# Sums of squares by VectorE and one ones matmul per half in the first stage of a decoder layer

## The chip, the cores and the metric

The kernel runs on one NeuronCore of a Trainium2 chip. The metric is the device time of one execution in microseconds (us). TensorE does matmuls, VectorE (DVE) and ScalarE (ACT) do elementwise work, GpSimd (POOL) does elementwise work on SBUF, and SyncE (SP) issues nearly all DMA transfers. Each engine runs its own instructions strictly in the order in which the program has them.

## The reference, cut to what matters

One layer: a token mixer with three branches and a ConvFFN after it, 1024 tokens of width 1024, all in float32. The change concerns only the start of the mixer: the RMS norm of the input and the first products with the input projection.

```python
def rms_norm(x, g):
    y = x * rsqrt(mean(x * x, axis=-1) + 1e-6)
    return y * g

h = rms_norm(x, norm_mix_pre)
z = h @ w_in                        # (1024, 7424), all branches from one projection
zr = z_rwkv + (token_shift(z_rwkv) - z_rwkv) * mu_shift
r, k, v, dw, da, dg = split(zr)     # 3 x 1024, 64, 64, 128 columns
w_log = -softplus(-(w0 + tanh(dw) @ w_up_decay)) - 0.5
a = sigmoid(a0 + da @ w_up_a)
g = sigmoid(dg) @ w_up_g
```

## The kernel before, in words

Everything lies transposed: channels on the 128 partitions, tokens along the row. x is held as eight tiles `xr[k]` of 128 channels x 1024 tokens, and the tokens are worked in two halves of 512 (`t0` = 0 and 512). A float32 operand of a matmul is split in two reduced parts: a rounded "high" part (`hh` of the input, `whi` of a weight) and the rest (`hl`, `wlo`). One product then takes three matmuls of 128x512 (`mm3`, L168 to L170): high by high, low by high, high by low. One projection of 128 columns (`gemm`) is 8 channel blocks of these, 24 matmuls into one PSUM bank. Banks come from the pool `psg` under two tags, `g0` and `g1`, two banks each; a weight's class `c` (0 or 1) says which tag, and also which SBUF buffers it uses (four each of `whi` and `wlo`, so one whole projection of 8 blocks, two blocks to a buffer).

The norm's factor 1/rms of a token is the same for all channels, so the first projections are taken from x * g without it, and the factor `xrs` is multiplied onto the PSUM result (`scaled`, L283) before it is evacuated (`shifted`, L309 to L315: ScalarE writes (1-mu) * z, VectorE adds mu times z shifted by a token). The sum over channels for the mean of squares runs over partitions: TensorE multiplies a 128x128 tile of 1/1024 (`ones`) in full float32 with the squares (`xsq`), block by block, into the bank `px` (L263). The profile shows such a full-float32 matmul as two instructions.

The function `start` runs the first stage in this order: `plain(0, first)` makes `hh` and `hl` of half 0, the squares, eight ones matmuls, and k and v of half 0 (the columns of heads 0 and 1), channel block by channel block; then the two small projections, decay and rate (`lu`, weight block 32) and gate (`gr`, block 33), of half 0; then `plain(512, after=last_mm[0])`, which has no projection: `hh`, `hl`, squares and eight ones matmuls of half 1; then `normed(0)`, which multiplies the factor onto x of half 0 and splits it anew; then decay, gate, k and v of half 1, for which the weights of k and v are loaded and split a second time. Then tanh and sigmoid, and the gate's own product: eight blocks p, each for both halves, three matmuls each (`gl`), copied out by ScalarE (`st`, L325) and stored to `d_g`. `normed(512)` comes last, tied to the copies. The code after it takes the next heads' k and v from the normed `hh` and `hl`.

The order on each engine is set by a scheduler that places the instructions by its own costs within what the code's dependences and the hints of `later` (an order without a wait) allow; so the rows on an engine are not simply the order of the code.

Of the kernel before, what the change touches and what calls it, by code (L numbers as in the profile page):

```python
# [9 lines left out]
F32 = mybir.dt.float32  # L10
FR = mybir.dt.float32r
AF = mybir.ActivationFunctionType
# [32 lines left out]
def trunk_kernel(ctx: ExitStack, tc: tile.TileContext, xT, memT, pvec, w_in, w_kv, w_upd, w_upg,  # L45
# [49 lines left out]
    for lo in (0, 64):  # L95
        s = slice(lo, lo + 64)
        V.tensor_scalar(cent[s], ident[s, lo:lo + 64], 1.0, -1.0 / 64, op0=ALU.mult, op1=ALU.add)
# [75 lines left out]
    def gemm(ws, rhs, width=512, behind=None, ps=None, log=None):  # L173
# [4 lines left out]
        for k in range(n):  # L178
# [3 lines left out]
            if log is not None:  # L182
                log.append(last_mm[0])
        return ps
# [58 lines left out]
    def plain(t0, ws=(), after=None):  # L243

        ts_ = slice(t0, t0 + 512)
        px = pss.tile([P, 512], F32, name="px", tag="s")
        pj = [psg.tile([P, 512], F32, name="psg", tag=f"g{w.c}") for w in ws]
        pin = phase[1][-1]
        for k in range(KC):
            x, hi = xr[k][:, ts_], hh[:, k, ts_]  # L250
            sq = wp.tile([P, 512], F32, name="xsq", tag="st", bufs=3)
            i = A.activation(hi, x, AF.Identity, scale=col("g_mix_pre", k))
            if t0:
                later(i, pin)
            V.scalar_tensor_tensor(hl[:, k, ts_], x, col("g_mix_pre", k), hi.bitcast(F32), op0=ALU.mult,
                                   op1=ALU.subtract)
            if k % 2 or t0:
                i = A.activation(sq, x, AF.Square)
                if t0:
                    later(i, pin)  # L260
            else:
                V.tensor_tensor(sq, x, x, op=ALU.mult)
            mm = PE.matmul(px, ones, sq, start=k == 0, stop=k == KC - 1)  # L263
            if after is not None:
                later(mm, after)
            for w, ps in zip(ws, pj):
                mm3(ps, w[k], (hi, hl[:, k, ts_]), k == 0, k == KC - 1)
        rstd(xrs_[:, ts_], px, 0)
        return pj

# [96 lines left out]
    def start():  # L367
# [5 lines left out]
        kv0 = rw.tile([P, 2, T], F32, name="kv0", tag="X00")  # L373
        SP.dma_start(gr[:, 1], w_upg)
        evs = [shifted(8, kv0[:, 0]), shifted(16, kv0[:, 1])]
        for ev, ps in zip(evs, plain(0, first)):
            scaled(ev, 0, ps)
        lo_ = [(shifted(24, u), load_w(w_in[32], KC, c=0)),
               (shifted(25, gr[:, 0]), load_w(w_in[33], KC, c=1))]
        for ev, ws in lo_:  # L380
            scaled(ev, 0, gemm(ws, hrhs(0)))
        hi_on_act[0] = False
        plain(512, after=last_mm[0])
        normed(0)
        for ev, ws in lo_:
            scaled(ev, 512, gemm(ws, hrhs(512)))
        for c, ev in enumerate(evs):
            scaled(ev, 512, gemm(load_w(w_in[16 + 8 * c], KC, c=c), hrhs(512)))
# [4 lines left out]
        act(gr[:, 0], gr[:, 0], AF.Sigmoid)  # L393
# [1273 lines left out]
```

## Time and profile before

| what | us |
|---|---|
| median of 3 runs | 2056.73 (2052.93 to 2056.75) |
| the profiled execution, its own time | 2058.67 |
| its span from the first to the last instruction | 2056.8 |
| TensorE busy | 2000.2 (97% of the span) |
| VectorE, ScalarE, GpSimd busy | 1378.4, 1073.6, 804.4 |

The mean granted TensorE clock of the execution is 0.995 of full speed. A time in a row of the profile counts from the start of the span. A row of the timeline gives start, duration, engine, line of the code, operation, output and inputs, a count, and in brackets the idle time of the engine before it with what ended it. The stage that is changed lies in the first 92 us of the span.

### The profile page before, as it was taken

How to read it: one execution, taken by the hardware profiler on the slowest of the kernel's cores; microseconds unless marked ns; L12 is line 12 of the kernel's file. 1: busy time of each engine (PE TensorE's matmuls, PEld its weight loads, DVE VectorE, ACT ScalarE, POOL GpSimd, SP SyncE). 2: the span in 40 equal slices, each digit the busy share in tenths (PEclk: the TensorE clock that was granted, in tenths of full speed). 3: DMA queues.
4: the chain of work that ended last, by engine and by line, in shares of the span. 5: the costliest groups of instructions: out<-in, count | busy, mean ns of one | idle time of the engine just before them, and what ended most of it. 6: DMA issues, size and time to landing. Idle time of an engine off the chain costs nothing. (4 is left out here: it accounts for less than half of the span.)

```text
span 2056.8 us, 34070 instructions
## 1 busy us (share of the span) xinstructions
PE 2000.2 (97%) x12246; PEld 1558.2 (76%) x12246; DVE 1378.4 (67%) x2204; ACT 1073.6 (52%) x2249; POOL 804.4 (39%) x883
## 2 busy tenths in 40 slices
PE   8999999999999999999999999999999999999997
PEld 5777767786778667776778887877678888877886
DVE  6567537663568357734596552768889888867798
ACT  7575338723773358434567343545544554444544
POOL 4521213121222121111122355655579888832441
PEclk9999999999999999999999999999999999999999
DMA  4412112120212121212525543645332222169776
GB/s 152 136 42 75 66 36 86 58 93 22 88 62 83 36 90 40 90 63 89 193 92 189 157 136 106 191 129 164 97 95 87 85 80 82 67 198 260 166 183 150
DMA packets 176714, 221.84 MB, mean 108 GB/s; under 512 B 16544, under 2 KB 128288, under 8 KB 176544
## 3 DMA queue, kind: packets, MB, share of 16 engines
q1 hardware_dynamic: 163616, 204.44, 30.7%
q0 software_dynamic: 11856, 14.16, 4.2%
q8 instruction: 97, 1.59, 0.3%
q10 hardware_dynamic: 1072, 1.05, 0.2%
q14 instruction: 73, 0.60, 0.1%
HBM read 170.30 MB, written 49.28 MB: 107 GB/s over the span
## 5 line engine op out<-in xcount | busy, mean ns | idle before, releaser
L132 POOL TENSOR_TENSOR wlo<-wraw,whi 128x256 fp32r<-128x256 f32 x472 | 412.7, 884 | 940.7 <-ACT whi L129 774.5
L168 PE MATMUL psg<-hh,whi 128*128 128x512 f32 x928 | 380.1, 410 | 2.6 <-DVE kv L315 2.6
L170 PE MATMUL psg<-hh,wlo 128*128 128x512 f32 x928 | 376.3, 406 | 0.4
L169 PE MATMUL psg<-hl,whi 128*128 128x512 f32 x928 | 375.5, 405 | 0.0
L129 ACT CAST whi<-wraw 128x256 fp32r<-128x256 f32 x472 | 182.5, 403 | 227.6 <-PE psg L169 105.7
L168 PEld LDWEIGHTS psg<-hh,whi 128*128 128x128 f32 x928 | 174.6, 188 | 43.1 <-DVE kv L315 3.8
L170 PEld LDWEIGHTS psg<-hh,wlo 128*128 128x128 f32 x928 | 174.2, 188 | 43.2 <-POOL wlo L132 5.9
L169 PEld LDWEIGHTS psg<-hl,whi 128*128 128x128 f32 x928 | 174.6, 188 | 39.4 <-issue 3.6
L1011 POOL TENSOR_TENSOR wt<-a,wt 128x256 fp32r<-128x256 f32 x136 | 156.7, 1176 | 35.6 <-ACT wt L1010 35.6
L168 PE MATMUL psd<-f,u 128*128 128x512 f32 x292 | 114.7, 393 | 3.1 <-ACT u L1405 2.4
L169 PE MATMUL psd<-f,u 128*128 128x512 f32 x292 | 114.6, 393 | 0.6 <-DVE f L1409 0.6
L170 PE MATMUL psd<-f,u 128*128 128x512 f32 x292 | 114.1, 392 | 0.0
L170 PE MATMUL psf<-h2h,wt 128*128 128x512 f32 x272 | 105.9, 389 | 1.0 <-POOL wt L1011 1.0
L169 PE MATMUL psf<-h2l,wt 128*128 128x512 f32 x272 | 105.8, 389 | 0.0
L168 PE MATMUL psf<-h2h,wt 128*128 128x512 f32 x272 | 105.8, 389 | 0.0
L1025 DVE SCALAR_TENSOR_TENSOR d<-z,pv,d 128x1023 f32<-128x1023 f32 x68 | 101.1, 1491 | 2.2
L1011 POOL TENSOR_TENSOR wt<-s,wt 128x256 fp32r<-128x256 f32 x68 | 80.3, 1201 | 3.4 <-ACT wt L1010 2.1
L686 DVE TENSOR_TENSOR HV<-ph,Hd 64x128 f32<-64x128 f32 x112 | 32.4, 289 | 72.2 <-PE ph L640 48.1
L168 PE MATMUL psf<-t,wt 128*128 128x512 f32 x204 | 79.4, 389 | 0.0
L169 PE MATMUL psf<-t,wt 128*128 128x512 f32 x204 | 79.4, 389 | 0.0
L170 PE MATMUL psf<-t,wt 128*128 128x512 f32 x204 | 79.4, 389 | 0.0
L1023 ACT ACTIVATE d<-z,pv 128x1024 f32<-128x1024 f32 x34 | 42.4, 1246 | 67.6 <-DVE z L1102 51.9
(425 smaller groups left out, 4747.0 us busy)
## 6 DMA issues: line engine op xcount, KB each, us to landing
wraw<-in_w_in SPq DMA_DIRECT2D x240, 128.0 KB, 2.4
a<-in_w_fup SPq DMA_DIRECT2D x128, 128.0 KB, 2.4
d_zg<-st SPq DMA_DIRECT2D x48, 256.0 KB, 2.7
wraw<-in_w_fup SPq DMA_DIRECT2D x80, 128.0 KB, 2.5
fw<-in_w_fdn SPq DMA_DIRECT2D x33, 256.0 KB, 4.3
fraw<-d_f SPq DMA_DIRECT2D x33, 256.0 KB, 4.5
wraw<-in_w_prwkv SPq DMA_DIRECT2D x64, 128.0 KB, 2.4
wraw<-in_w_o SPq DMA_DIRECT2D x64, 128.0 KB, 2.5
```

What stands on the lines that cost most here:

```text
L129: last_whi[0] = A.copy(hi, src).ins
L132: (V if lo_on_dve[0] else G).tensor_tensor(lo, src, hi.bitcast(F32), op=ALU.subtract)
L168: first = PE.matmul(ps, wh, xh, start=start, stop=False)
L169: PE.matmul(ps, wh, xl, start=False, stop=False)
L170: last_mm[0] = PE.matmul(ps, wl, xh, start=False, stop=stop).ins
L686: ready = V.tensor_tensor(HV[q, :, c + 1, e], ph[q], Hd[q], op=ALU.add).ins
L1011: low = eng.tensor_tensor(w[1][:, us], src[u], w[0][:, us].bitcast(F32), op=ALU.subtract)
L1023: A.activation(d, z, AF.Identity, scale=col("cw2", j), bias=col("cb", j))
L1025: V.scalar_tensor_tensor(d[:, n:], z[:, :T - n], col(cw, j), d[:, n:], op0=ALU.mult, op1=ALU.add)
```

## The change

Three things are changed in the first stage.

1. The squares of the eight channel blocks are added up by VectorE into a tile `xsum`, one per half, and one ones matmul per half takes the sum over partitions (`x_norm`). Before there were eight ones matmuls per half.
2. k and v are taken from the unnormed operand in both halves (`plain(512, first, ...)`), before gate and decay, with the weights still in SBUF. The norm's factor of half 0 is made after channel block 3 of half 1 (`amid`), that of half 1 after block 3 of the gate projection of half 0. Gate now comes before decay.
3. The gate's sigmoid and split are done for each half by itself, the gate's products run over half 0 first, and both `normed` come after. The table of ScalarE functions for the sigmoid is loaded once, after the second norm factor. The tile `cent` is made later in the code.

```diff
-    def plain(t0, ws=(), after=None):
+    def plain(t0, ws, sum_, amid=None):
 
         ts_ = slice(t0, t0 + 512)
-        px = pss.tile([P, 512], F32, name="px", tag="s")
         pj = [psg.tile([P, 512], F32, name="psg", tag=f"g{w.c}") for w in ws]
-        pin = phase[1][-1]
         for k in range(KC):
             x, hi = xr[k][:, ts_], hh[:, k, ts_]
-            sq = wp.tile([P, 512], F32, name="xsq", tag="st", bufs=3)
-            i = A.activation(hi, x, AF.Identity, scale=col("g_mix_pre", k))
-            if t0:
-                later(i, pin)
+            sq = wp.tile([P, 512], F32, name="xsq", tag="st", bufs=3) if k else sum_
+            A.activation(hi, x, AF.Identity, scale=col("g_mix_pre", k))
             V.scalar_tensor_tensor(hl[:, k, ts_], x, col("g_mix_pre", k), hi.bitcast(F32), op0=ALU.mult,
                                    op1=ALU.subtract)
             if k % 2 or t0:
-                i = A.activation(sq, x, AF.Square)
-                if t0:
-                    later(i, pin)
+                A.activation(sq, x, AF.Square)
             else:
                 V.tensor_tensor(sq, x, x, op=ALU.mult)
-            mm = PE.matmul(px, ones, sq, start=k == 0, stop=k == KC - 1)
-            if after is not None:
-                later(mm, after)
+            if k:
+                V.tensor_tensor(sum_, sum_, sq, op=ALU.add)
             for w, ps in zip(ws, pj):
                 mm3(ps, w[k], (hi, hl[:, k, ts_]), k == 0, k == KC - 1)
-        rstd(xrs_[:, ts_], px, 0)
+            if amid is not None and k == 3:
+                amid()
         return pj
+
+    def x_norm(t0, sum_):
+        px = pss.tile([P, 512], F32, name="px", tag="s")
+        later(PE.matmul(px, ones, sum_, start=True, stop=True), last_mm[0])
+        rstd(xrs_[:, t0:t0 + 512], px, 0)
...
         kv0 = rw.tile([P, 2, T], F32, name="kv0", tag="X00")
+        sums = rw.tile([P, 2, 512], F32, name="xsum", tag="X10")
+        evs = [shifted(8, kv0[:, 0]), shifted(16, kv0[:, 1])]
+        made = {}
+
+        def kv_done(n, t0):
+            x_norm(t0, sums[:, n])
+            for ev, ps in zip(evs, made[n]):
+                scaled(ev, t0, ps)
+
+        made[0] = plain(0, first, sums[:, 0])
+        made[1] = plain(512, first, sums[:, 1], partial(kv_done, 0, 0))
         SP.dma_start(gr[:, 1], w_upg)
-        evs = [shifted(8, kv0[:, 0]), shifted(16, kv0[:, 1])]
-        for ev, ps in zip(evs, plain(0, first)):
-            scaled(ev, 0, ps)
-        lo_ = [(shifted(24, u), load_w(w_in[32], KC, c=0)),
-               (shifted(25, gr[:, 0]), load_w(w_in[33], KC, c=1))]
-        for ev, ws in lo_:
-            scaled(ev, 0, gemm(ws, hrhs(0)))
+        lo_ = [(shifted(25, gr[:, 0]), load_w(w_in[33], KC, c=1)),
+               (shifted(24, u), load_w(w_in[32], KC, c=0))]
         hi_on_act[0] = False
-        plain(512, after=last_mm[0])
+        split_w(gr[:, 1], gl[:, 2], gl[:, 3])
+
+        def gate(t0):
+            s = slice(t0, t0 + 512)
+            act(gr[:, 0, s], gr[:, 0, s], AF.Sigmoid)
+            split(gr[:, 0, s], gl[:, 0, s], gl[:, 1, s])
+
+        for t0, _ in HALVES:
+            for n, (ev, ws) in enumerate(lo_):
+                asked = partial(kv_done, 1, 512) if n == 0 and t0 == 0 else None
+                scaled(ev, t0, gemm(ws, hrhs(t0), amid=asked))
+                if asked:
+                    table(SIGMOID)
+                if n == 0:
+                    gate(t0)
+        for t0, _ in HALVES:
+            for p in range(8):
+                ps_ = slice(p * P, (p + 1) * P)
+                ws = Ws([(gl[:, 2, ps_], gl[:, 3, ps_])])
+                ws.c = 1
+                spilled(d_g[p])(t0, gemm(ws, lambda k: (gl[:, 0, t0:t0 + 512], gl[:, 1, t0:t0 + 512])))
         normed(0)
-        for ev, ws in lo_:
-            scaled(ev, 512, gemm(ws, hrhs(512)))
-        for c, ev in enumerate(evs):
-            scaled(ev, 512, gemm(load_w(w_in[16 + 8 * c], KC, c=c), hrhs(512)))
+        normed(512, spills)
```

How the change moves instructions is shown at three places. From the matmul that stands next on TensorE behind 268 projection and gate matmuls (the kernel before starts it at 91.69 us) the order of both programs is the same on TensorE; ahead of it both have the same 268 and differ in the ones matmuls and the order.

First, TensorE where the half 1 ones matmuls stood. Before, behind the last matmuls of gate's half 0 (bank `psg_408`) and ahead of decay's half 1 (`psg_504`):

```order
L170 MATMUL psg_408<-hh_143,wlo_375 128x512
L263 MATMUL px_437<-xsq_438,ones_85 128x512
L263 MATMUL px_437<-xsq_443,ones_85 128x512
L263 MATMUL px_437<-xsq_448,ones_85 128x512
L263 MATMUL px_437<-xsq_453,ones_85 128x512
L263 MATMUL px_437<-xsq_458,ones_85 128x512
L263 MATMUL px_437<-xsq_463,ones_85 128x512
L263 MATMUL px_437<-xsq_468,ones_85 128x512
L263 MATMUL px_437<-xsq_473,ones_85 128x512
L168 MATMUL psg_504<-hh_143,whi_331 128x512
```

And now, at the seam from v of half 1 (`psg_314`) to gate of half 0 (`psg_466`), up to that gemm's second block pair:

```order
L165 MATMUL psg_314<-hh_141,whi_196 128x512
L166 MATMUL psg_314<-hl_142,whi_196 128x512
L167 MATMUL psg_314<-hh_141,wlo_197 128x512
L165 MATMUL psg_466<-hh_141,whi_416 128x512
L166 MATMUL psg_466<-hl_142,whi_416 128x512
L167 MATMUL psg_466<-hh_141,wlo_417 128x512
```

The eight ones matmuls in a row are gone; gate of half 0 follows v of half 1 at once, and its bank is one of the two of tag `g1`, both of which v's halves still hold. The two remaining ones matmuls stand inside gemms, behind block 3.

Second, VectorE in the same stretch. Before, from the last blocks of half 0 to the first evacuation:

```order
L255 SCALAR_TENSOR_TENSOR hl<-xr_147,pv,hh 128x512 x4
L262 TENSOR_TENSOR xsq<-xr_147 128x512
L283 TENSOR_TENSOR psg<-psg,xrs 128x512 x2
L274 SCALAR_TENSOR_TENSOR xr_145<-xr_145,pv,xrs 128x512
L311 COPY zc<-psg 128x1
L315 SCALAR_TENSOR_TENSOR kv_224<-psg,pv,kv_224 128x511
```

And now, from the last blocks of half 1 to the first evacuation (`xr_145` is here the tile of blocks 4 to 7):

```order
L257 TENSOR_TENSOR xsum<-xsum,xsq 128x512
L250 SCALAR_TENSOR_TENSOR hl<-xr_145,pv,hh 128x512
L257 TENSOR_TENSOR xsum<-xsum,xsq 128x512
L744 TENSOR_SCALAR cent<-ident 64x64
L281 TENSOR_TENSOR psg<-psg,xrs 128x512 x2
L272 SCALAR_TENSOR_TENSOR xr_143<-xr_143,pv,xrs 128x512
L309 COPY zc<-psg 128x1
L313 SCALAR_TENSOR_TENSOR kv_221<-psg,pv,kv_221 128x511
```

The evacuation of k and v of half 0 moved behind all sixteen `hl` of both halves and the fourteen additions; half of `cent` stands there too.

Third, ScalarE while the gate's products are copied out. Before:

```order
L325 COPY st<-psg 128x512 x2
L277 CAST hh<-xr_146 128x512
L325 COPY st<-psg 128x512 x2
L277 CAST hh<-xr_146 128x512
```

And now:

```order
L323 COPY st<-psg 128x512 x2
L275 CAST hh<-xr_144 128x512
L412 CAST ld<-lu 64x1024
L323 COPY st<-psg 128x512
L412 CAST la<-lu 64x1024
L323 COPY st<-psg 128x512 x2
L275 CAST hh<-xr_144 128x512
L434 ACTIVATE sp<-kv_221,pv 128x512
L323 COPY st<-psg 128x512
```

The tanh, the two casts of its result and the squares `sp` of the next step, which stood ahead of the gate's copies, now stand between them.

More of the change, by code (lines that the diff above doesn't have):

```diff
@@ L94, in trunk_kernel @@
     smask = const.tile([P, 512], F32, name="smask")
-    for lo in (0, 64):
-        s = slice(lo, lo + 64)
-        V.tensor_scalar(cent[s], ident[s, lo:lo + 64], 1.0, -1.0 / 64, op0=ALU.mult, op1=ALU.add)
     G.memset(mstrict, 1.0)
@@ L171, in mm3, with gemm @@
         return first
-    def gemm(ws, rhs, width=512, behind=None, ps=None, log=None):
+    def gemm(ws, rhs, width=512, behind=None, ps=None, log=None, amid=None):
         if ps is None:
@@ L257, in plain @@
             if k % 2 or t0:
-                i = A.activation(sq, x, AF.Square)
-                if t0:
-                    later(i, pin)
+                A.activation(sq, x, AF.Square)
             else:
                 V.tensor_tensor(sq, x, x, op=ALU.mult)
-            mm = PE.matmul(px, ones, sq, start=k == 0, stop=k == KC - 1)
-            if after is not None:
-                later(mm, after)
+            if k:
+                V.tensor_tensor(sum_, sum_, sq, op=ALU.add)
             for w, ps in zip(ws, pj):
                 mm3(ps, w[k], (hi, hl[:, k, ts_]), k == 0, k == KC - 1)
-        rstd(xrs_[:, ts_], px, 0)
-        return pj
+            if amid is not None and k == 3:
+                amid()
+        return pj
+    def x_norm(t0, sum_):
+        px = pss.tile([P, 512], F32, name="px", tag="s")
+        later(PE.matmul(px, ones, sum_, start=True, stop=True), last_mm[0])
+        rstd(xrs_[:, t0:t0 + 512], px, 0)
     def normed(t0, behind=None):
@@ L392, in start @@
             V.tensor_tensor(l[o], u[q], l[q].bitcast(F32), op=ALU.subtract)
-        act(gr[:, 0], gr[:, 0], AF.Sigmoid)
-        split(gr[:, 0], gl[:, 0], gl[:, 1])
-        split_w(gr[:, 1], gl[:, 2], gl[:, 3])
-        for p in range(8):
-            ps_ = slice(p * P, (p + 1) * P)
-            ws = Ws([(gl[:, 2, ps_], gl[:, 3, ps_])])
-            ws.c = 1
-            ev = spilled(d_g[p])
-            for t0, _ in HALVES:
-                ev(t0, gemm(ws, lambda k: (gl[:, 0, t0:t0 + 512], gl[:, 1, t0:t0 + 512])))
-        normed(512, spills)
         return kv0
@@ L729, in fill_to @@
         return filled[n - 1]
-    table(SIGMOID)
     first_kv = start()
+    for lo in (0, 64):
+        s = slice(lo, lo + 64)
+        V.tensor_scalar(cent[s], ident[s, lo:lo + 64], 1.0, -1.0 / 64, op0=ALU.mult, op1=ALU.add)
     kv = group_kv(0, [first_kv])
```

## The prediction

> **What bounds the kernel now.** I read the page first, for the engine that is never free.
>
> ```profile
> PE 2000.2 (97%) x12246; PEld 1558.2 (76%) x12246; DVE 1378.4 (67%) x2204; ACT 1073.6 (52%) x2249; POOL 804.4 (39%) x883
> ```
>
> TensorE is busy 97% of the span, so whatever time its stream gains or loses at the start moves all that follows. The page's slices are 51 us wide and too coarse for the stage, so next I cut it at the points where TensorE's work changes kind: half 0 with its ones matmuls, the half 1 ones matmuls, the 96 matmuls of half 1, the seam to the gate, and on to 91.69, the first matmul that stands alike in both programs.
>
> ```profile
> core 0: us, PE busy (x) PEld busy (x) DVE busy (x) ACT busy (x) POOL busy (x), PEclk, DMA share, GB/s
> 5.31:36.74 31.43, 30.89 (x112) 21.76 (x113) 18.04 (x26) 21.28 (x41) 17.83 (x20) 1.00 0.67 221
> 36.74:47.41 10.67, 8.43 (x17) 3.38 (x16) 10.48 (x19) 9.60 (x17) 0.00 (x0) 0.84 0.01 2
> 47.41:69.75 22.34, 22.34 (x98) 18.00 (x97) 19.20 (x25) 12.50 (x16) 19.26 (x24) 1.00 0.20 59
> 69.75:75.30 5.55, 2.15 (x8) 1.23 (x7) 3.26 (x4) 3.80 (x9) 3.32 (x5) 1.00 0.33 96
> 75.30:91.69 16.39, 16.39 (x70) 12.75 (x70) 6.38 (x11) 12.97 (x24) 0.27 (x1) 1.00 0.66 240
> ```
>
> Two stretches hold no projection work or little: 10.67 us in which only ones matmuls run, and 5.55 us at the seam to the gate with 2.15 busy. The timeline says what they are made of.
>
> ```profile
> 16.83 1.02 PE L263 MATMUL px<-xsq,ones 128*128 128x512 f32 x2
> 19.08 1.02 PE L263 MATMUL px<-xsq,ones 128*128 128x512 f32 x2
> 41.72 6.25 PE L263 MATMUL px<-xsq,ones 128*128 128x512 f32 x10 [2.24 <-ACT xsq L258]
> 71.20 0.50 PE L169 MATMUL psg<-gl 128*128 128x512 f32 x1 [0.95 <-DVE gl L123]
> 75.30 0.50 PE L168 MATMUL psg<-gl 128*128 128x512 f32 x1 [2.45 <-ACT st L325]
> 97.58 0.39 PE L168 MATMUL psg<-hh,whi 128*128 128x512 f32 x1
> 104.38 0.39 PE L168 MATMUL psg<-hh,whi 128*128 128x512 f32 x1
> ```
>
> From 97.58 to 104.38 thirty matmuls start: 0.2267 us each. From 16.83 to 19.08 go six of them (1.36) and one ones matmul, two instructions: 0.89. The block from 36.74 is eight of these, 7.1 us, and 3.5 us in which TensorE waits for ScalarE's squares.
>
> **What is removed.** Fourteen ones matmuls, 14 x 0.89 = 12.5 us of TensorE; the 3.5 us of waiting in their block; and at the seam 5.55 less eight matmuls (1.8), 3.7 us, if the gate's operand is ready in time. That is 19.7 us, and no more can be won. Four of the five table loads after the first also go, and the second load and split of the weights of k and v: eight transfers and eight pairs on POOL, all beside the path, where SP and POOL waited for room.
>
> **What is paid: VectorE feeds TensorE.** The fourteen additions go to the engine that makes `hl`, which every second matmul of a block waits for.
>
> ```profile
> L255 DVE SCALAR_TENSOR_TENSOR hl<-xr,pv,hh 128x512 fp32r<-128x512 f32 x16 | 12.9, 836 | 3.9 <-ACT hh L252 3.7
> L262 DVE TENSOR_TENSOR xsq<-xr 128x512 f32<-128x512 f32 x4 | 3.3, 822 | 1.0 <-DMA xr<-in_xT 1.0
> L97 DVE TENSOR_SCALAR cent<-ident 64x64 f32<-64x64 f32 x2 | 1.7, 830 | 0.0
> 8.99 0.75 DVE L255 SCALAR_TENSOR_TENSOR hl<-xr,pv,hh 128x512 fp32r<-128x512 f32 x1 [2.94 <-ACT hh L252]
> 9.66 0.68 DVE L262 TENSOR_TENSOR xsq<-xr 128x512 f32<-128x512 f32 x1
> 10.26 0.74 DVE L255 SCALAR_TENSOR_TENSOR hl<-xr,pv,hh 128x512 fp32r<-128x512 f32 x1
> 13.30 1.23 DVE L262 TENSOR_TENSOR xsq<-xr 128x512 f32<-128x512 f32 x1
> 14.45 4.16 DVE L255 SCALAR_TENSOR_TENSOR hl<-xr,pv,hh 128x512 fp32r<-128x512 f32 x4
> 37.46 2.07 DVE L255 SCALAR_TENSOR_TENSOR hl<-xr,pv,hh 128x512 fp32r<-128x512 f32 x3
> 12.83 4.57 POOL L132 TENSOR_TENSOR wlo<-wraw,whi 128x256 fp32r<-128x256 f32 x4 [0.28 <-ACT whi L129]
> ```
>
> No addition of SBUF tiles of this size is in the trace; the nearest row is the square, also a tensor by tensor of 128x512. Up to 8.99 nothing changes (the second block of x lands then). From there to the last `hl` of half 1 the order has 15 `hl`, 3 squares, 13 additions and one `cent`. At the means, 15 x 0.836 + 16 x 0.822 + 0.83 = 26.5 us: the last `hl` is ready at 35.5. The bounds lie in the rows below: start to start, with POOL idle, `hl` takes 2.07 / 3 = 0.69 and the square 10.26 - 9.66 = 0.60, which gives 20.8 us; beside POOL's `wlo` `hl` takes 4.16 / 4 = 1.04 and one square 1.23, which gives 36.1 us. I take the means, since in the new stretch POOL works about half the time (the splits of k and v, `gl` and the splits for gate and decay).
>
> The Trainium skill says why the two sets of rows differ, in "GPSIMD Engine Reference", Specifications: POOL shares its SBUF interfaces with VectorE and meets "contention with DVE instructions in a 2-port perf mode or with two SBUF inputs". Each addition has two SBUF inputs, so by this rule the change adds work of the exposed kind; the 1.04 against 0.69 agrees. By it alone the sum would lie toward the upper bound.
>
> Five matmuls follow the last `hl`: TensorE is through with k and v at 36.6, where before (36.74) it had done as many projection matmuls, k, v, decay and gate of half 0.
>
> **What is paid: the bank.** Gate of half 0 needs a bank of tag `g1`, and both are v's. It is freed by a chain on VectorE behind the last addition.
>
> ```profile
> 28.87 1.30 DVE L283 TENSOR_TENSOR psg<-psg,xrs 128x512 f32<-128x512 f32 x2 [9.65 <-ACT xrs L200]
> 31.91 0.73 DVE L315 SCALAR_TENSOR_TENSOR kv<-psg,pv,kv 128x511 f32<-128x511 f32 x1
> 10.31 5.14 SPq L234 DMA_DIRECT2D xr<-in_xT  x9
> DMA to landing us min/median/max: 3.2/5.7/6.0
> L274 DVE SCALAR_TENSOR_TENSOR xr<-xr,pv,xrs 128x512 f32<-128x512 f32 x16 | 13.1, 857 | 0.0
> ```
>
> Before, the same chain (two `scaled`, one `xr`, two evacuations) runs from 28.87 to 32.64, 3.77 us. Now: last addition 35.5 + 0.8, `cent` 0.8, chain 3.8: the bank is free at 40.9, and TensorE idles 4.3 us; everything on TensorE is queued behind it. What is late next? The factor itself is not: half 0's sum is complete by 8.99 + 8 `hl` + 10 others + `cent`, about 25, and ScalarE is through with half 1 some three blocks ahead of VectorE, since it has three buffers of squares. Nor is x: the last transfer is issued by 15.5 and lands by 21.5. Seven `xr` (7 x 0.857 = 6.0) stand ahead of the second evacuation: 40.9 + 6.0 + 3.8 = 50.7, and its bank is wanted only by half 1 of gate, from 53.6.
>
> **Gate and decay.** 96 matmuls, 21.8 us, one ones matmul, 0.9, and the clock.
>
> ```profile
> 40.00:45.00 5.00, 3.28 (x5) 1.35 (x6) 5.00 (x10) 3.95 (x9) 0.00 (x0) 0.79 0.01 3
> 45.00:50.00 5.00, 5.00 (x16) 3.03 (x15) 4.26 (x7) 4.82 (x7) 0.63 (x2) 0.87 0.00 0
> 75.00:80.00 5.00, 4.70 (x18) 3.25 (x19) 1.64 (x4) 3.73 (x8) 0.57 (x1) 1.00 0.59 209
> ```
>
> After the idle 2.24 us the granted clock was 0.79 and 0.87 for two windows, 5 x 0.21 + 5 x 0.13 = 1.7 us; after the 2.45 at the seam it stayed 1.00. I take 0.9, with 0 and 1.7 as ends. So 40.9 + 21.8 + 0.9 + 0.9 = 64.5.
>
> The page "TensorE: Matmul & The Clock Gate" of the Trainium skill, in Part 1, gives half rate after an idle window of about 3.4 us and full rate again after about as long a busy one; that would be an estimated 1.7 for the new gap. The gap of 2.24 with its 0.79 fits it only loosely.
>
> **The gate's stage.** 76 matmuls stand between there and 91.69's instruction: 17.2 us. The gate's operand took 8.9 us from its scaling (62.23) to its split (69.73 + 1.41); now half 0's comes to 50.7 + 8.9 = 59.6, before 64.5, and half 1's to 68, while eight products and ten matmuls of the next k fill up to 72. So the 3.7 us do go.
>
> ```profile
> 62.23 0.69 DVE L283 TENSOR_TENSOR psg<-psg,xrs 128x512 f32<-128x512 f32 x1
> 69.73 1.41 DVE L123 TENSOR_TENSOR gl<-gr,gl 128x1024 fp32r<-128x1024 f32 x1 [1.34 <-ACT gl L122]
> L325 ACT COPY st<-psg 128x512 f32<-128x512 f32 x16 | 9.3, 588 | 3.4 <-PE psg L170 2.8 <-DMA d_g<-st 0.5
> L277 ACT CAST hh<-xr 128x512 fp32r<-128x512 f32 x16 | 9.4, 618 | 0.0
> L424 ACT ACTIVATE sp<-kv,pv 128x512 fp32r<-128x512 f32 x2 | 1.4, 722 | 0.9 <-DVE gl L123 0.6 <-DVE kv L315 0.3
> L200 ACT ACTIVATE lu<-lu 64x1024 f32<-64x1024 f32 x1 | 1.1, 1060 | 2.1 <-DVE lu L315 2.1
> L391 ACT CAST la<-lu 64x1024 fp32r<-64x1024 f32 x1 | 1.1, 1051 | 0.0
> L309 ACT ACTIVATE lu<-psg,omu 128x512 f32<-128x512 f32 x2 | 1.4, 679 | 3.6 <-DVE psg L283 3.6
> ```
>
> But ScalarE, which empties the banks, now has more between the copies: 16 x 0.588 + 8 x 0.618 + 2 x 0.722 + 1.06 + 2 x 1.05 + 2 x 0.68 = 20.3 us. Neighbours overlap by up to 0.1, some 3 us over thirty, so the wait beyond TensorE's 17.2 is between 0 and 3.1; I take 1.5. That ends the stage at 64.5 + 17.2 + 1.5 = 83.2.
>
> **The sum.** 91.69 - 83.2 = 8.5 us earlier, and behind it TensorE's order is unchanged: 19.7 removed, and paid back 11.2, mostly by the wait for `hl` and for the bank. The profiled execution would go from 2058.67 to 2050.2. The median of the runs, 2056.73, lies 1.9 below that execution; from it, 2048.2. A measurement of this kernel tells about 0.2%, 4.1 us, from no change.
>
> **The rivals.**
>
> 1. VectorE runs free of POOL. At the lower bound the last `hl` comes 5.7 earlier, gain 14.2, time 2042.5. For it: POOL's weight splits of k and v for half 1 are gone, and it waits for buffers that TensorE holds. Against it: in half 0 the rows with 1.04 stand in just this stretch. Chance 0.24.
> 2. VectorE is contended throughout. The last `hl` comes 9.6 later, and all of the gain is eaten: loss 1.1, time 2057.8, no change that can be measured. For it: denser work on VectorE meets POOL more often, and one of the four squares was slow. Against it: POOL was idle from 17.4 to 22.3, for `gl`'s weights landed no earlier. Chance 0.18, most of it for something between this and the forecast.
> 3. Slower: TensorE's clock. Fed block by block with short gaps from 9 to 36 us and then left idle for 4.3, TensorE is granted half speed and stays there while the banks of tag `g1` let it start and stop. It decides where the loss exceeds 8.5 + 4.1 = 12.6 us, which is 25 us of wall time at half speed; for all of gate and decay, 21.8 more, the time would be 2070.0. For it: 0.79 and 0.87 after one gap. Against it: 1.00 in the 31.43 us of half 0, gaps and all, and 1.00 behind the seam. Chance 0.05.
>
> For rival 3 there is a rule in "TensorE: Matmul & The Clock Gate", under "A second HAM failure mode: psum-queue depth-cycling": small gaps between groups of matmuls make the clock swing between half and full. The rows of half 0 do not show it.
>
> **How the numbers follow.** The forecast has 0.53, with 2044.8 to 2051.6 as its own range (its ends for clock and gate's stage, -2.4 and +2.4, and 1 us on VectorE). Reaching into rival 1 and rival 2 until two in ten are left gives 2043.0 to 2053.5. Faster by over 0.2%, below 2052.6: nearly all of the forecast (0.51), rival 1 (0.24), a part of rival 2 (0.05), 0.80. Slower, above 2060.8: most of rival 3 and a tail of rival 2, 0.05. The rest, 0.15, is no change.
>
> **What would show it.** In the profile after: the last `hl` of half 1 near 35.5 (30 for rival 1, 45 for rival 2); one idle gap of TensorE near 4 us ended by an evacuation of VectorE; 1.00 or a little less as granted clock in the 20 us behind it; no wait for `gl`; waits for `st` of ScalarE of 1 to 3 us in all in the gate's stage; and the instruction of 91.69 near 83. The prediction is wrong if the additions cost clearly more or less than a square, if a second bank wait appears at half 1 of gate, or if a gain at 83 is not there at the end of the span.

## The result, and the profile after

| | median, us | ratio to before (95% interval) |
|---|---|---|
| before | 2056.17 (2052.93 to 2056.75) | |
| after | 2061.15 (2059.32 to 2063.41) | 1.0023 (1.0012 to 1.0033) |

The change makes the kernel slower by 0.23%, 5 us, where 8.5 us of gain were predicted. The profiled execution of after took 2063.41 us, its span is 2061.7, the mean granted clock 0.992.

The waits of TensorE in the first 100 us of after (engine and line, what it waited for, us in total, times, longest) name the cause at once:

```profile
PE psg L167 <- POOL wlo L129: 14.7, 1, 14.7
PE psg L165 <- ACT whi L126: 5.9, 1, 5.9
PE psg L165 <- ACT st L323: 3.3, 2, 2.6
```

The 5.9 us are the start of the program, where TensorE waits 5.3 us in before. New is one wait of 14.7 us, and it is for POOL, not for VectorE. The timelines of POOL, VectorE and TensorE around it:

```profile
10.55 2.28 POOL L129 TENSOR_TENSOR wlo<-wraw,whi 128x256 fp32r<-128x256 f32 x2 [3.12 <-ACT whi L126]
12.77 0.31 POOL L352 MEMSET ulo<- 128x256 f32 x1
13.04 20.12 POOL L129 TENSOR_TENSOR wlo<-wraw,whi 128x256 fp32r<-128x256 f32 x4
```

```profile
11.01 1.23 DVE L255 TENSOR_TENSOR xsq<-xr 128x512 f32<-128x512 f32 x1
12.16 0.96 DVE L744 TENSOR_SCALAR cent<-ident 64x64 f32<-64x64 f32 x1
12.80 0.74 DVE L250 SCALAR_TENSOR_TENSOR hl<-xr,pv,hh 128x512 fp32r<-128x512 f32 x1
13.46 0.68 DVE L257 TENSOR_TENSOR xsum<-xsum,xsq 128x512 f32<-128x512 f32 x1
14.07 0.73 DVE L250 SCALAR_TENSOR_TENSOR hl<-xr,pv,hh 128x512 fp32r<-128x512 f32 x1
...
29.18 0.73 DVE L250 SCALAR_TENSOR_TENSOR hl<-xr,pv,hh 128x512 fp32r<-128x512 f32 x1
29.84 0.67 DVE L257 TENSOR_TENSOR xsum<-xsum,xsq 128x512 f32<-128x512 f32 x1
30.53 0.62 DVE L744 TENSOR_SCALAR cent<-ident 64x64 f32<-64x64 f32 x1
```

```profile
31.16 0.79 PE L167 MATMUL psg<-hh,wlo 128*128 128x512 f32 x1 [14.70 <-POOL wlo L129]
```

The two `wlo` before 12.8 take 1.14 us each, and VectorE's square beside them 1.23: the engines take turns, one instruction of each, as in before. Then POOL's next `wlo` starts at 13.04 and VectorE runs 27 more instructions back to back, every `hl` in 0.73 and every addition in 0.67, as if POOL were not there. Of the 20.12 us of the four `wlo` the first takes 18.06, the greatest of the three times in the group's row (least, median, greatest, in ns); it ends when VectorE's row ends:

```profile
L129 POOL TENSOR_TENSOR wlo<-wraw,whi x6: 719/932/18060, 10.5 to 32.4; 128x256 fp32r<-128x256 f32 x6
```

The three behind it take 0.7 each. TensorE, which needs that `wlo` for blocks 4 and 5, stands from 16.46 to 31.16.

By stage, in the same columns as before (cut at the wait's end, the start of gate, of the gate's own product, and at the instruction that stood at 91.69):

```profile
core 0: us, PE busy (x) PEld busy (x) DVE busy (x) ACT busy (x) POOL busy (x), PEclk, DMA share, GB/s
5.31:31.16 25.85, 10.29 (x27) 7.04 (x27) 22.65 (x35) 19.07 (x35) 22.08 (x8) 0.80 0.58 205
31.16:49.64 18.48, 18.48 (x72) 14.67 (x73) 3.87 (x8) 5.13 (x11) 10.18 (x12) 0.91 0.24 73
49.64:72.40 22.76, 22.76 (x100) 18.46 (x100) 22.73 (x36) 13.39 (x24) 9.56 (x11) 1.00 0.14 41
72.40:94.42 22.02, 18.68 (x77) 13.79 (x76) 13.21 (x19) 17.75 (x31) 3.69 (x4) 1.00 0.50 180
```

k and v are done at 49.64, not 36.6; gate follows without a gap, and the common instruction stands at 94.42, 2.7 us later than in before. In the last stage TensorE waits twice for `st`, the copies by ScalarE that empty the banks (before: 2.45 us once for `st`, 0.95 for `gl`):

```profile
76.95 0.50 PE L165 MATMUL psg<-gl 128*128 128x512 f32 x1 [2.58 <-ACT st L323]
83.39 0.50 PE L165 MATMUL psg<-gl 128*128 128x512 f32 x1 [0.74 <-ACT st L323]
75.71 0.72 ACT L434 ACTIVATE sp<-kv,pv 128x512 fp32r<-128x512 f32 x1 [2.47 <-DVE gl L120]
```

ScalarE's `sp` waits 2.47 us for VectorE; the copies `st` are queued behind it, and TensorE waits for them. From the common instruction on the offset is 2.7, from 110 us 3.2, and still 3.2 at 1000 us. Later it wanders (5.4 at 1600, 4.5 at the last matmul); two executions with the same order of instructions do that as well (the last experiment), so it is not put down to the change.

### The profile page after: what moved, and what is told of

Same layout as the page of the kernel before. It is cut to its first block, busy times and chain, and to the rows that moved or that the text cites. A ratio compares the mean times of both kernels' runs of the same rounds, so it can differ in the third digit from the quotient of the medians.

```text
span 2061.7 us, 33989 instructions
## 1 busy us (share of the span) xinstructions
PE 1990.4 (97%) x12218; PEld 1555.0 (75%) x12218; DVE 1385.4 (67%) x2219; ACT 1067.5 (52%) x2246; POOL 809.6 (39%) x867
## 4 chain that ended last, share of the span: by engine, by line
PE 37%; DVE 6%; DMA 5%; ACT 1%; issue 1%; POOL 1%; SPq 1%; ACTq 0%; POOLq 0%; DVEq 0%
PE psg L165 5%; PE psg L167 5%; PE psg L166 5%; PE psf L167 5%; PE psf L165 5%; PE psf L166 5%; PE psd L166 2%; PE psd L167 2%; PE psd L165 2%; DMA R<-d_f 1%; DMA g<-d_zg 1%; POOL wlo L129 1%; DMA fw<-in_w_fdn 1%; DMA wraw<-in_w_o 0%; DVE h2l L120 0%
## 5 line engine op out<-in xcount | busy, mean ns | idle before, releaser
L129 POOL TENSOR_TENSOR wlo<-wraw,whi 128x256 fp32r<-128x256 f32 x464 | 422.2, 920 | 958.1 <-ACT whi L126 789.6
L167 PE MATMUL psg<-hh,wlo 128*128 128x512 f32 x928 | 378.0, 408 | 15.2 <-POOL wlo L129 14.7
L1023 POOL TENSOR_TENSOR wt<-a,wt 128x256 fp32r<-128x256 f32 x136 | 157.1, 1180 | 36.6 <-ACT wt L1022 36.6
```

The costliest lines, as they stand in the source:

```text
L129: (V if lo_on_dve[0] else G).tensor_tensor(lo, src, hi.bitcast(F32), op=ALU.subtract)
L167: last_mm[0] = PE.matmul(ps, wl, xh, start=False, stop=stop).ins
L1023: low = eng.tensor_tensor(w[1][:, us], src[u], w[0][:, us].bitcast(F32), op=ALU.subtract)
```

## The experiments

One number is given for each kernel besides its time: by how much the common instruction behind the stage comes earlier or later than in before ("shift", after: +2.7). It is read just behind the stage, in one execution of each kernel.

The first theory, A in the expectations: an unbroken row on VectorE, with the additions in it, keeps POOL out of its operands. Its rivals: POOL is late for a reason of its own (B), or the new order is to blame (C).

### POOL's part given to VectorE

```diff
-    hi_on_act[0] = True
+    hi_on_act[0] = lo_on_dve[0] = True
     first = [Ws(), Ws()]
```

> The changed kernel, with the low halves (wlo) of the eight pairs of k and v weight tiles made by VectorE in place of POOL, which then has no such work in the first stage. Theory A, VectorE's unbroken row of hl, square and addition keeps POOL out of its operands (one wlo took 18.06 us in the changed kernel, and TensorE waited 14.7 us for it): with POOL's part gone the wait goes too, VectorE gets eight instructions of about 0.42 us more (3.4 us), k and v are done at about 38 us instead of 49.6, the common instruction is at 83 to 85 us instead of 94.4, and the time is about 2050 us (2048 to 2053). Theory B, POOL is late for a reason of its own (a transfer, its queue) and the loss lies in the new order or in the half clock: VectorE's added work and the order hold TensorE up as before, k and v are not done before 46 us, and the time is 2058 us or more.

2048.81 us, ratio 0.9962 (0.9947 to 0.9976), shift -9.7. The long wait is gone and the rest of TensorE's waiting is for `hl`:

```profile
PE psg L166 <- DVE hl L251: 3.5, 5, 1.8
```

So POOL's `wlo` is where the time was lost; a late transfer or the order, in which B saw the loss, is not the cause. That POOL might be slow for a reason of its own, without VectorE, this run can't exclude; the exchange of two numbers below does. This and the next variant are the fastest complete kernels here; both beat before and after. A variant with only the last four `wlo` on VectorE did as well within the intervals:

> The changed kernel with the low halves of only the last four pairs of k and v weight tiles made by VectorE, those that POOL made in the 20.12 us of its stall; the first four stay with POOL, which has them done at 12.8 us in the changed kernel. If the stalled wlo are all that the first stage lost: the wait of 14.7 us goes as with all eight on VectorE (2048.81 us), and VectorE, with 1.7 us less to do, hands over hl up to 1.7 us earlier; time 2046 to 2049 us. If VectorE's row is what holds TensorE there, time as with all eight or later, 2049 to 2051 us.

2049.49 us, 0.9972 (0.9960 to 0.9983), shift -8.5. The two are not told apart, so whether VectorE's extra 1.7 us cost anything stays open. In this variant TensorE waits 3.1 us for `wlo` of the next projections; where that comes from is told below.

### No additions

```diff
-            if k:
-                V.tensor_tensor(sum_, sum_, sq, op=ALU.add)
```

> The changed kernel without the 14 additions of squares on VectorE: the ones matmul takes the square of block 0 alone, so the norm's sum is left incomplete; everything else stays in its place. Theory A in its narrow form (the additions, in place on one tile, are what closes the row; hl and square alone change places with POOL as in the kernel before, 1.2 us and 1.15 us): no wlo over 3 us, TensorE's wait of 14.7 us under 3 us, k and v done at 36 to 39 us, time 2046 to 2050 us. Theory A in its wide form (any unbroken row on VectorE keeps POOL out): wlo waits until VectorE's row ends, which is then 9.4 us earlier (14 times 0.67), so TensorE still waits about 5 us, time about 2052 us. Theory B (POOL late for a reason of its own): the wait stays near 14 us, time 2058 us or more.

2046.85 us, 0.9956 (0.9941 to 0.9970), shift -13.0. No `wlo` is long (the least, median and greatest time in ns stand behind the count):

```profile
L129 POOL TENSOR_TENSOR wlo<-wraw,whi x13: 734/1145/1269, 10.2 to 32.7; 128x256 fp32r<-128x256 f32 x13
```

That was the narrow form of A. The next two should have confirmed it, and the second did not.

### The order alone, and the sum alone

The order of after with the sixteen ones matmuls and no additions:

> The change with its other part alone: k and v of both halves first, gate and decay after them, the gate's operand in halves, but the 16 ones matmuls and no additions. Theory A: POOL gets its turns (wlo about 1.2 us each), TensorE has no wait over 4 us for wlo; the 14 matmuls come back (12.5 us), so that k and v are done at about 46 to 50 us and the common instruction is at 90 to 95 us, time 2052 to 2060 us, no or a small gain. Theory C (the order causes the loss): TensorE waits over 10 us for wlo as in the changed kernel, and with the ones matmuls on top the time is 2070 us or more.

2052.85 us, 0.9974 (0.9961 to 0.9986), shift -6.9, longest `wlo` 1.19 us: the order is not the cause, and alone it gains. The kernel before with the additions and one ones matmul for a half, in its old order:

> The kernel before with one part of the change alone: squares added up on VectorE and one ones matmul for a half, the order of the stage as before (gate and decay between the halves, whole gate operand). Theory A: the additions in half 0 shut POOL out here too while VectorE's row lasts; half 0 alone has 8 hl, 4 squares and 7 additions, and half 1's 8 hl and 7 additions follow in the queue, so a wlo of more than 8 us stands in the trace, TensorE waits 8 to 15 us for it, and what the 14 ones matmuls save (12.5 us) is lost again: 2054 to 2062 us. Theory C (the loss comes from the new order, not from the additions): POOL goes on in turns of 1.2 us, the ones matmuls' 12.5 us come off at least by half, 2044 to 2050 us.

2059.06 us, 1.0011 (1.0000 to 1.0022), shift -0.8. TensorE loses time at the seam, but not to POOL:

```profile
L132 POOL TENSOR_TENSOR wlo<-wraw,whi x12: 731/740/1198, 9.9 to 32.9; 128x256 fp32r<-128x256 f32 x12
72.65 0.79 PE L168 MATMUL psg<-gl 128*128 128x512 f32 x1 [5.08 <-ACT gl L122]
```

Half 0 has all its additions here, among the same `hl` and squares, and every `wlo` gets its turn. A had expected one of more than 8 us. Neither part locks POOL out by itself; both together do, or so it seemed here.

### Which rows lock POOL out

Rows of VectorE without the kernel around them, in fourteen stretches:

> Not the kernel but a measurement of its own, in fourteen stretches: in each VectorE has 24 instructions of 128x512 in an unbroken row, and POOL four wlo of 128x256 that come free a few instructions into it (one of 0.73 us when nothing else runs). The row is, in turn: hl alone; hl and square by turns; hl and addition in place; hl and addition in place as the three-operand form; hl and addition into the other of two tiles; hl and an addition whose operands nothing in the row writes; additions in place alone; then the same seven in reverse order. Nothing of the reference is computed here. Theory W (any unbroken row keeps POOL out): the first wlo lasts 10 us or more in every stretch. Theory N (the addition that reads what VectorE has just written keeps POOL out): about 1.2 us for each wlo in the stretches of hl and of hl and square, and in those with free additions, 10 us or more in the stretches with sums in place. Theory R (it hangs on the instant at which POOL asks, not on the kind): long and short ones in the same kind of stretch, or none longer than 2 us at all.

```profile
L65 POOL TENSOR_TENSOR wlo<-w,whi x56: 725/1167/1327, 8.3 to 277.6; 128x256 fp32r<-128x256 f32 x56
```

None of 56 is longer than 1.33 us, with additions or without, in place or not. Theories W and N fall; R, the instant, is left. The kernel with the additions in another form:

```diff
-                V.tensor_tensor(sum_, sum_, sq, op=ALU.add)
+                V.scalar_tensor_tensor(sum_, sq, 1.0, sum_, op0=ALU.mult, op1=ALU.add)
```

> The changed kernel with the 14 additions written in the three-operand form (square times 1.0 plus the sum) that hl has, which hands POOL its turn in the kernel before; same operands, same places. If the form of the instruction decides: wlo at most 1.3 us, TensorE's wait of 14.7 us gone, k and v done at 36 to 40 us, time 2047 to 2051 us. If reading the sum that was just written, or the unbroken row as such, decides: a wlo of 10 us or more again, time 2058 to 2064 us.

```profile
L129 POOL TENSOR_TENSOR wlo<-wraw,whi x6: 717/934/18053, 10.1 to 32.0; 128x256 fp32r<-128x256 f32 x6
```

2061.75 us, 1.0031 (1.0021 to 1.0040), shift +2.0: 18.05 us again. The form is not it. Something small on VectorE, so that it yields for an instant:

```diff
+                if not t0:
+                    turn = V.memset(turn_, 0.0)
+                    later(turn, add.ins)
+                    behind.append(turn.ins)
```

> The changed kernel with one small instruction more behind each addition of half 0 on VectorE: a memset of 128x1 into a tile that nothing reads (7 of them). Theory A with the lock passed on only where VectorE's next instruction does not ask for it: POOL gets in at each memset, wlo at most 2 us, TensorE's wait under 4 us, time 2047 to 2051 us. If POOL needs a real pause, or is late for another reason: one wlo of 10 us or more stays, time 2059 us or more.

2052.69 us, 0.9988 (0.9978 to 0.9997), shift -4.9, longest `wlo` in the row 1.6 us. That looked like a cure, but the scheduler had moved something else with it: `cent`, a constant of 128x64 that VectorE makes in two instructions of 64x64, one for partitions 0 to 63 and one for 64 to 127. In this kernel both halves run together at 12.05 and 13.04. Side by side, all traces agree: in after and in the three-operand kernel one half of `cent` stands ahead of the row and the other behind it; in before, without additions, with the order alone, with the sum alone and here both stand together; with all `wlo` on VectorE they come at 67.9; with the last four there, one half stands ahead too, but none of POOL's `wlo` for k and v is left to wait. There it is the next instruction of POOL that stands, the first step of splitting the gate's weights, which takes 1.04 to 1.40 us in every other kernel:

```profile
21.53 10.33 POOL L128 TENSOR_SCALAR gl<-gr 128x1024 fp32r<-128x1024 f32 x1 [9.37 <-DMA gr<-in_w_upg]
```

POOL asked for it 10 us after that half of `cent`, and it ends at 31.85, when VectorE's row of `hl` and additions is over (30.9) and a microsecond of its own has passed; the `wlo` that TensorE waited 3.1 us for stand behind it. So most of the first experiments had changed a second thing, and the new theory, K, is that one half of `cent` alone ahead of the row locks POOL out.

### cent

The lines of `cent` back where before has them, all else as in the change:

> The changed kernel with one edit of it undone, the smallest: the two lines that make cent (the two halves of a 128x64 constant, 64x64 each, on VectorE) stand again where the kernel before has them, so that both halves run together, ahead of the row of hl and additions, in place of one ahead of it and one behind it. All additions and the new order stay. Theory K (what locks POOL out is how the row begins: one half of cent alone, hl right behind it while POOL still runs its memset of ulo, as in the three kernels where it was seen or where VectorE ran a shade faster, 0.735 us for an hl in place of 0.745): wlo at most 1.3 us, no wait of TensorE over 4 us for it, time 2046 to 2051 us. Theory A (the unbroken row with additions as such): a wlo of 10 us or more and 14 us of waiting again, 2058 to 2064 us.

2053.02 us, 0.9990 (0.9978 to 1.0002), shift -5.2. No `wlo` is long, and TensorE's waits are of the kinds that the prediction had priced:

```profile
PE psg L169 <- DVE hl L253: 4.5, 4, 1.8
PE psg L168 <- ACT st L326: 2.6, 1, 2.6
PE psg L168 <- DVE kv L316: 1.5, 1, 1.5
...
35.52 1.23 DVE L253 SCALAR_TENSOR_TENSOR hl<-xr,pv,hh 128x512 fp32r<-128x512 f32 x1
...
41.35 0.47 PE L168 MATMUL psg<-hh,whi 128*128 128x512 f32 x1 [1.53 <-DVE kv L316]
```

With `cent` split as in the change, but without POOL's memset between the `wlo`:

```diff
-    G.memset(ulo2.bitcast(F32), 0.0)
+    V.memset(ulo2.bitcast(F32), 0.0)
```

> The changed kernel with the memset of ulo (128x256, POOL, between its fourth and fifth wlo) moved to VectorE, which runs it at the start of the program; cent stays split. If the overlap of POOL's memset with the start of an hl is the trigger: the long wlo is gone, time 2046 to 2051 us. If one half of cent ahead of the row is: the fifth wlo lasts 10 us or more as before, time 2058 to 2064 us. Theory A in general: as the latter.

2061.54 us, 1.0022 (1.0010 to 1.0034), shift +4.5, one `wlo` of 18.20 us. The memset has no part in it. And both halves behind the whole row:

> The changed kernel with both halves of cent made behind the last hl of the second normalisation, so that none of it stands in or ahead of VectorE's row of hl, squares and additions; all else as in the change. If the half of cent ahead of the row is the trigger: wlo at most 1.3 us, no wait of TensorE over 4 us for them, the common instruction about 5 us earlier than before, time 2048 to 2053 us (2053.02 with both halves ahead of the row). If the row itself locks POOL out and the halves together only happened to open it: a wlo of 10 us or more, 2058 to 2064 us.

```profile
PE psg L165 <- DVE kv L315: 3.1, 1, 3.1
PE psg L166 <- DVE hl L250: 3.1, 4, 1.8
```

2052.18 us, 0.9984 (0.9974 to 0.9993), shift -4.3, no wait for `wlo`. The row does not lock POOL out when no half of `cent` stands ahead of it.

### Which half

Stretches by themselves once more, with single pieces in the row:

> A measurement of its own again, in sixteen stretches, nothing of the reference computed: VectorE's row of 26 hl and additions in place, POOL with five wlo of 128x256 beside it; in the row, four instructions in, stand by turns: one half of cent (64x64) with a memset of 128x256 on POOL ahead of its third wlo; both halves with the memset; no cent with the memset; one half without the memset; neither; a whole 128x64 instruction with the memset; one half and the memset in a row of hl alone; a copy of 64x64 with the memset. Then the eight again with the piece one instruction earlier. Theory K: a wlo of 10 us or more in the stretches with one half (with the memset, or without it too), about 1.2 us in those with none or both. If no stretch shows one over 2 us, the trigger is not in these pieces alone.

Two of the sixteen stretches lock POOL out, both with the half on partitions 0 to 63, one of them in a row of `hl` alone. In the six others with a single piece on these partitions nothing happens. One of each kind:

```profile
L84 POOL TENSOR_TENSOR wlo<-w,whi x5: 720/914/14577, 9.1 to 26.6; 128x256 fp32r<-128x256 f32 x5
L63 DVE TENSOR_SCALAR cent<-x x2: 604/654/704, 11.4 to 26.0; 64x64 f32<-64x64 f32 x2
...
L84 POOL TENSOR_TENSOR wlo<-w,whi x5: 1165/1168/1968, 85.3 to 90.6; 128x256 fp32r<-128x256 f32 x5
L63 DVE TENSOR_SCALAR cent<-x x2: 182/187/192, 86.5 to 104.6; 64x64 f32<-64x64 f32 x2
```

The difference stands in the row of `cent`: 0.70 us where POOL was locked out, 0.18 where it was not (in all six). In the first case it stood 0.5 us behind a `wlo` of POOL. So the instant counts, and the next measurement puts the piece where the engines surely change places:

> A measurement of its own, sixteen stretches, nothing of the reference computed: VectorE's row of 30 hl and additions in place, POOL with eight wlo of 128x256 beside it, no memset on POOL. Eight instructions into the row, where the two engines should be changing places, stands one small piece: cent's operation on partitions 0 to 63 (64x64); on partitions 64 to 127; on all (128x64); the first and the second half behind each other; a copy of 64x64; a memset of 64x64; a sum of two operands of 64x64; nothing. Then the eight again with the piece one instruction later, ahead of an addition. If an instruction with one operand that itself had to wait for POOL is the trigger (a wlo of 14.577 us stood behind such a half of cent): a wlo of 10 us or more in the stretches with half 0, half 1, all and perhaps the copy, not with the sum of two operands, the memset or nothing. If it is the partitions 0 to 63 alone: with half 0, not with half 1, all, or half 1 behind half 0. If it needs an exact instant too: in one of the two rounds only, or in none.

The eight `wlo` of five stretches of the first round, in order: partitions 0 to 63; 64 to 127; all; a copy on 0 to 63; a sum of two operands on 0 to 63.

```profile
L86 POOL TENSOR_TENSOR wlo<-w,whi x8: 722/1168/14582, 9.1 to 16.5; 128x256 fp32r<-128x256 f32 x8
L86 POOL TENSOR_TENSOR wlo<-w,whi x8: 720/1167/1867, 41.0 to 49.2; 128x256 fp32r<-128x256 f32 x8
L86 POOL TENSOR_TENSOR wlo<-w,whi x8: 720/1168/1869, 72.0 to 80.1; 128x256 fp32r<-128x256 f32 x8
...
L86 POOL TENSOR_TENSOR wlo<-w,whi x8: 716/1166/14579, 134.0 to 156.0; 128x256 fp32r<-128x256 f32 x8
...
L86 POOL TENSOR_TENSOR wlo<-w,whi x8: 717/1166/14612, 197.0 to 219.0; 128x256 fp32r<-128x256 f32 x8
```

Over both rounds: the three pieces on partitions 0 to 63 lock POOL out in six of six stretches (13.9 to 14.6 us, to the end of the row), whatever the operation; the half on 64 to 127, all partitions, the second half behind the first, the memset and nothing at all in none of ten (longest 1.87). With operation and instant alike, the partitions decide. They are not all of it: the memset also wrote 0 to 63 alone, but took 0.11 us and so did not stand behind a `wlo`, and the six pieces of the first measurement that took 0.18 did not either.

### Two numbers exchanged

If that is what cost the change its time, the other half first must cure it, with no instruction moved on any engine:

```diff
-    for lo in (0, 64):
+    for lo in (64, 0):
         s = slice(lo, lo + 64)
         V.tensor_scalar(cent[s], ident[s, lo:lo + 64], 1.0, -1.0 / 64, op0=ALU.mult, op1=ALU.add)
```

> The changed kernel with two numbers exchanged: cent's half on partitions 64 to 127 is made first and the one on 0 to 63 second, so that every engine has the same instructions in the same places as in the change, and only the partitions of two 64x64 instructions differ. If an instruction of VectorE on partitions 0 to 63 alone, at a change of turns, is what locks POOL out (six of six stretches with such a piece had a wlo of 13.9 to 14.6 us, none of the ten others had one over 1.9): no wlo over 1.3 us in the row, the wait of 14.7 us gone, the time as with cent behind the row, 2050 to 2054 us. If the row, the single half or its instant does it: a wlo of 18 us again and 2058 to 2064 us.

```profile
12.64 1.87 POOL L129 TENSOR_TENSOR wlo<-wraw,whi 128x256 fp32r<-128x256 f32 x2
...
39.83 6.83 POOL L129 TENSOR_TENSOR wlo<-wraw,whi 128x256 fp32r<-128x256 f32 x3 [1.75 <-ACT whi L126]
...
12.75 1.17 DVE L250 SCALAR_TENSOR_TENSOR hl<-xr,pv,hh 128x512 fp32r<-128x512 f32 x1
```

The row that took 20.12 us for four `wlo` is gone, TensorE's wait with it, and VectorE pays its turns again (1.17 where it had 0.74). 2055.45 us, 1.0003 (0.9994 to 1.0011), shift -2.2. The time is 1.5 us over the expected range. The half on 0 to 63 now stands at 37.41, ahead of a row of `xr`, and three `wlo` beside it take 6.83 us (the last of them 5.27, to the end of that row), where with `cent` behind they took 2.85: the lock-out has come back in another place. But TensorE waits only 0.2 us for `wlo` here, so that is not where the time went. TensorE stood 3.75 us for the bank (3.12 with `cent` behind), was granted 0.54 and 0.78 of the clock from 40 to 45 and 45 to 50 us (0.66 and 1.00), and took 25.4 us for gate and decay (24.4). The counter-test, the same exchange in the kernel before:

> The kernel before with the same two numbers exchanged: the half on partitions 0 to 63 comes second, right ahead of VectorE's row of hl and squares, at 11.7 us. If partitions 0 to 63 lock POOL out: one wlo lasts from about 12.8 us to the end of VectorE's row, which without POOL's turns is at about 17 us, so 4 us or more, TensorE waits for it by some 2 to 4 us, and the time is 2 to 5 us over the kernel before. If not: as before.

```profile
L132 POOL TENSOR_TENSOR wlo<-wraw,whi x14: 720/741/2702, 9.9 to 33.0; 128x256 fp32r<-128x256 f32 x14
```

The lock-out comes, but for 2.70 us only: POOL gets in after the row's fourth instruction, though three more follow. The fifth, an `hl` at 14.35, is the first whose `hh` was ready no more than 0.05 us before it (at 14.30; 0.52 or more for the others), so VectorE's row seems to have paused there for ScalarE; in after every `hl` behind `cent` had 1.4 us or more. Time 2054.81, 1.0000 (0.9990 to 1.0011): the expected loss of 2 to 5 us does not come. How long VectorE's row goes on without a pause decides what a lock-out costs.

This kernel has before's order on every engine, and yet its shift goes from -0.5 behind the stage to -5.0 at 1600 us with an unchanged median: the late wandering belongs to the execution. One difference stays open: in all thirteen kernels the ratio, taken as us, lies on the slower side of the shift, by 0.1 to 4.4 us and by 2.3 on average (after: shift +2.7, ratio about +4.7). Whether something is lost behind the stage, or the one traced execution of before was late in it, no run here shows.

## Why the prediction was wrong

**The step that failed is "What is paid: VectorE feeds TensorE".** It asked how much POOL slows VectorE, put the moved `cent` at 0.83 us of VectorE's time, and put TensorE's wait for POOL's `wlo` at nothing, without a reason. The price was on that side: `cent` split by the scheduler, its half on partitions 0 to 63 alone ahead of a long row, shut POOL out for 18.06 us, and TensorE waited 14.7 us. VectorE itself ran at the lower bound (last `hl` done at 29.9; bounds 29.8 and 45.1). That was rival 1's condition, with the opposite result, since what it saved on VectorE, POOL and then TensorE paid. Taken away by the exchange of two numbers, the loss of 0.23% is gone (1.0023 to 1.0003); with `cent` behind the row the ratio is 0.9984. The exchange shows the cause of the loss; it does not bring the gain that was forecast, for which see the gate's stage below.

**The sum, term by term.** The common instruction came 11.2 us later than forecast (94.42 for 83.2): gate began 8.7 late (49.64 for 40.9), gate and decay took 22.76 for 23.6, the gate's stage 22.02 for 18.7.

**VectorE's time and the bank** were right where POOL is not locked out: last `hl` done at 36.7 with `cent` together (35.5 forecast), gate of half 0 begins at 41.35, behind an evacuation of VectorE (40.9 forecast; 41.0 with `cent` behind, 41.6 with the halves exchanged).

**Gate and decay.** Right within 0.8 in after, but not as forecast: the idle gap at the bank, for which the 0.9 was put in, is not there, and the clock was 1.00. Where the gap came, the price was higher: 24.4 us behind 3.12 idle, 25.4 behind 3.75 (22.8 behind 1.53, at 1.00).

**The gate's stage was mis-sized by 3.3 us.** "So the 3.7 us do go" is wrong. Before took as long for the same 76 matmuls (columns as above):

```profile
69.75:91.69 21.94, 18.54 (x78) 13.99 (x77) 9.64 (x15) 16.77 (x32) 3.59 (x5) 1.00 0.57 204
```

After took 22.02, and the other kernels in the new order took 21.7 to 23.0; only the order alone, with its sixteen ones matmuls, has 19.3. The gate's operand is in time, but the waits for `st` are 3.3 us, not 1.5: I added up ScalarE's busy time and did not see that its queue stands still for 2.47 us at `sp`. (The same waits for `st` are 2.4 to 3.6 us in the other kernels of this order, 1.1 with the ones matmuls; `sp` waits 2.5 us with `cent` together and behind too.) The other 1.5 us lie in matmuls that start more than 0.23 us apart; why stays open. With the lock-out away this stage is what the forecast lacks: with `cent` together it took 22.3 us for 18.7, and the shift is -5.2 where -8.5 was forecast.

**What is removed.** The matmuls go, but the additions take about as much: without lock-out the full change has 0.9984 (0.9974 to 0.9993), the order alone 0.9974 (0.9961 to 0.9986), the sum alone 1.0011 (1.0000 to 1.0022). The intervals of the first two overlap; the shifts say the same (-4.3, -6.9, -0.8). So what gains is the order. The order with neither additions nor those ones matmuls (its norm incomplete) has 0.9956, shift -13.0.

**Rival 3**, the clock, was not the mechanism. Half clock (0.54 between 20 and 35 us) came as a consequence of the wait; at 0.91 over the 18.48 us behind it that is some 1.7 us.

**The rule behind the two sets of rows.** The prediction cited the Trainium skill, "GPSIMD Engine Reference", Specifications, for contention that would slow VectorE. The Trainium skill's page "SBUF — State Buffer", section "SBUF: two separate sides", states how it is settled: the shared ports are an exclusive lock, and whoever starts first has it "for the whole instruction; the other fully blocks". The turns agree (1.17 for a `wlo` of 0.72 beside a row). Who has it next the section does not say; if the lock changed hands at the end of each instruction, the `wlo` of 13.04 would have had its turn when the `hl` of 12.80 ended, at 13.54. It took until 31.10, and here the measurement decides.

## What to carry to other kernels

Where VectorE and POOL work side by side, price both directions: look in the trace for one POOL instruction that lasts many times its usual time beside a VectorE row at its undisturbed pace. Do not place a VectorE instruction on partitions 0 to 63 alone ahead of a long unbroken row while POOL has work that someone waits for; let the half on 64 to 127 follow it, or keep such constants away. And when experiments on parts of a change disagree, list everything that the scheduler moved in each before believing the part that was edited.

## What the hardware showed

A VectorE instruction of 64x64 on partitions 0 to 63 that had itself to stand behind a `wlo` lets VectorE's following row run without a turn for POOL: one POOL instruction then lasted 18.06, 18.05 and 18.20 us in three kernels, 10.33 in a fourth, where POOL asked only 10 us after the piece, and 13.9 to 15.2 us in eight stretches of bare rows. The same on partitions 64 to 127, on all, or on 0 to 63 and then 64 to 127 never did, and neither did a piece on 0 to 63 that had not to wait (0.18 us, or 0.11 for a memset). In the bare rows it was seen with one operand, two operands and a copy, in a row of `hl` alone and in one with additions; it ended with the row, and in one kernel after four instructions, where the row seems to have paused. A turn of POOL in between need not end it: with the halves exchanged, two `wlo` of 0.75 and 0.73 us ran beside VectorE instructions that read PSUM, and the third, beside the row of `xr`, lasted 5.27. That POOL's instruction waits for a lock on the shared ports is inferred from its length and from VectorE's undisturbed pace; why the partitions matter, and what exactly ends it, no run here shows.
